# A two-block kernel: order of projections and indexer, place of the attention's halves, and the first tile's indexer queries

## Chip, cores and metric

The kernel runs as one program on one core of a Trainium2 chip. The metric is the device time of that core in microseconds (us), the median of three runs.

## What is computed

The reference is a chain of two transformer blocks on 512 tokens of width 1024, all in float32, with a final norm. The change lies in the attention of the first block and in what follows it up to the output projection:

```python
proj = rms_norm(h, norm1_g) @ w_in
q, k, v, qi, ki, wi, su, sv, ga, gb = split_columns(proj)
# dsa_attention, for each query:
rel = relu(einsum('bqhd,bsd->bqhs', qi, ki))       # the indexer: 8 heads of 64
score = einsum('bqh,bqhs->bqs', wi, rel)
score = where(causal, score, -inf)
_, sel = top_k(score, 128)                         # 128 = 512 // 4 keys for a query
logits = where(valid, q . k[sel] * 128 ** -0.5, -inf)
y_attn = softmax(logits) @ v[sel]
merged = sigmoid(ga) * (y_sgu @ w_branch_a) + sigmoid(gb) * (y_attn @ w_branch_b)
h = h + merged @ w_out
```

The queries of tokens 0 to 127 have at most 128 keys before them, so for them the selection takes every causal key. A mixture-of-experts layer, a second attention block (stick-breaking and linear attention) and a second mixture of experts follow; the change does not touch how they are computed.

## The kernel before

Four tiles of 128 tokens (t or i from 0 to 3) make up the 512 tokens. The program is a sequence of four stages: the first dense block (`dense1`), its experts, the second dense block, its experts and the final norm. A scheduler puts each engine's instructions in an order by their place in the program and by when it thinks they can run; each engine then works through its own list in order. Nothing jumps a queue on the chip.

In `dense1` each float32 product is made of three matmuls on high and low halves (`mm3`, lines 145 to 148): high by high, high by low, low by high. A projection takes 512 columns (or 256, or 328) of `w_in`: four chunks of 2 x 128 rows come by DMA from SP's queue into four raw buffers (`wr`), ACT rounds each to its high half (`wh`, L135), and VectorE, or GpSimd for the chunks listed in `POOLED`, subtracts to get the low half (`wl`, L138). TensorE then runs 4 tiles x 2 x 3 matmuls on each chunk, 96 for a projection, into four PSUM banks. What is done with the result is passed in as `evac`; for queries and keys it is the rope (L323 to L329, VectorE) and four transposes a tile (L504).

The order of these steps is written out by hand in `ORDER_A` (L32). q, k and V are projections of half the heads each (0 or 1). I0 and I1 are the indexer's projections: `ev_qi` (L445) rotates four heads' queries, transposes them and splits them into `qih` and `qil`; I1 also makes the keys `kih`, `kil` and the heads' weights `wi`. C1 to C3 are `choose(i)` (L467) for tile i: for each of 8 heads three score matmuls into one of three PSUM banks (`sp`), a Relu on ACT (L480), and an accumulation on VectorE (L477 for the first head, L481 for seven); then a causal mask on GpSimd (L483), 16 rounds on VectorE of maximum (L487) and replacement (L488), which take out 8 keys each, and a compare (L489) that writes the mask M[i]. There is no C0; M[0] is only causal. S0 and S1 are the gating unit's values, with statistics on VectorE (L568), H the attention heads, U and G further projections.

After the steps come the gating unit, branch a, the gate projection `sgb` and branch b. Branch b reads the attention's output as halves `yah`, `yal` in the pool `d1ya`: eight copies on ACT (L662) and eight subtractions on GpSimd (L663). Ahead of them in the program stands `later`, which loads vectors and calls `clear_rows` (L745): it fills a tile with zeros and copies it by two DMAs of GpSimd's queue over the two arrays `yd` in DRAM, which the experts later add to. That tile and a table of positions (`jp`) share a small temporary pool:

```python
with tc.tile_pool(name="gtmp", bufs=1, side="right", reuse_waits="tile") as tmp:
    front_consts(K, g, position_gap(K, tmp, pool_op), pool_op)
    clear_rows(K, tmp, pool_op)
```

The pool is placed at the right end of what is free. In a partition `jp` takes 512 bytes and the zeros 4096; a tile that is put where another one was waits for the readers of the old one.

Of the kernel before, what the change touches and what calls it, by code (L numbers as in the profile page):

```python
# [10 lines left out]
F32 = mybir.dt.float32  # L11
# [6 lines left out]
ALU = mybir.AluOpType  # L18
# [4 lines left out]
D = 1024  # L23
NT = T // 128
KD = D // 128
# [3 lines left out]
POOLED = (0, 1, 2) + tuple(range(16, 32))  # L29
LEFT1, LEFT2 = 3, 0  # L30
LAST1, LAST2 = 0, 3
ORDER_A = ("q0 I0 R I1 q1 C1 C2 V0 k0 C3 S0 S1 V1 H00 H01 H02 k1 H03 U0 H10 H11 H12 G0 H13 U1")  # L32
ORDER1 = ("turned",) * 2, ("logged",) * 2, ("logged",) * 2, ("ranked",) * 2
ORDER2 = ("last", "turned"), ("logged",) * 2, ("logged", "ranked"), ("ranked",) * 2
RING1, RING2 = 12, 15
# [4 lines left out]
def f32(ap):  # L40
    return ap.bitcast(F32)
# [10 lines left out]
def after(K, x, y):  # L52

    K.tc.add_manual_dep(x.ins, y.ins.name, mybir.DependencyInfo(mybir.DependencyClass.NoSync,
                                                                mybir.DependencyReason.DATA), reason="order")
# [12 lines left out]
def rsqrt(K, pool, a, n, name, keep=None):  # L68

    nc = K.nc  # L70

    def t_(role, dt=F32):
        return pool.tile([128, n], dt, name=f"{name}{role}", tag=f"rsq{n}{role}", bufs=2)

    sh = t_("s", I32)
    nc.vector.tensor_scalar(sh, a.bitcast(I32), 1, None, op0=ALU.logical_shift_right)
    yi = t_("i", I32)
    nc.vector.tensor_scalar(yi, sh, -1.0, float(0x5F3759DF), op0=ALU.mult, op1=ALU.add)
    y, c = yi.bitcast(F32), 1.0
    for i in range(3):  # L80

        t = t_(f"t{i}")
        if n == 1:
            nc.vector.tensor_scalar(t, y, y, a, op0=ALU.mult, op1=ALU.mult)
        else:
            nc.vector.tensor_mul(t, y, y)
            nc.vector.tensor_mul(t, t, a)
        y2 = keep if i == 2 and keep is not None else t_(f"y{i}")
        if i < 2:
            nc.vector.scalar_tensor_tensor(y2, t, 3.0 * c * c, y, op0=ALU.subtract, op1=ALU.mult)  # L90
            c = -2.0 * c ** 3
        else:
            nc.vector.tensor_scalar(t, t, -0.5 / c ** 3, 1.5 / c, op0=ALU.mult, op1=ALU.add)
            nc.vector.tensor_mul(y2, y, t)
        y = y2
    return y
# [12 lines left out]
class WStream:  # L109
# [18 lines left out]
    def split(self, raw, nk, n, into=None):  # L128
        nc, pool = self.K.nc, self.pool
        if into is None:  # L130
            wh = pool.tile([128, nk, n], F32R, name=f"wh{self.i}", tag="wh", bufs=self.nb)
            wl = pool.tile([128, nk, n], F32R, name=f"wl{self.i}", tag="wl", bufs=self.nb)
        else:
            wh, wl = into
        self.high = nc.scalar.activation(wh, raw, AF.Copy)  # L135
        pooled = self.i in self.pooled
        low = nc.gpsimd if pooled else nc.vector
        self.low = low.tensor_tensor(wl, raw, f32(wh), op=ALU.subtract)  # L138
        if pooled:
            self.pool_low = self.low  # L140
        self.i += 1
        return wh, wl


def mm3(nc, out, ah, al, bh, bl, first, last):
    nc.tensor.matmul(out, ah, bh, start=first, stop=False)  # L146
    nc.tensor.matmul(out, al, bh, start=False, stop=False)  # L147
    return nc.tensor.matmul(out, ah, bl, start=False, stop=last)  # L148
# [9 lines left out]
        return self.pool.tile(shape, dt, name=name, tag=self.tag, bufs=self.n)  # L158


def proj_tok(K, W, acc_pool, src, c0, n, xh, xl, evac):

    nc = K.nc
    accs = [acc_pool.tile([128, 512], F32, name=f"acc{t}", tag="acc", bufs=4) for t in range(NT)]
    for kc in range(4):
        raw = W.load(src, c0, n, 2 * kc, 2)
        wh, wl = W.split(raw, 2, n)
        for t in range(NT):
            for k in range(2):
                kk = kc * 2 + k  # L170
                mm3(nc, accs[t][:, :n], xh[:, kk, t * 128:(t + 1) * 128], xl[:, kk, t * 128:(t + 1) * 128],
                    wh[:, k, :], wl[:, k, :], kk == 0, kk == KD - 1)
            if kc == 3:
                evac(t, accs[t])

# [134 lines left out]
def rope(K, work, src, t, heads, half, name, out=None):  # L310

    nc = K.nc
    step = 64 // half
    cs = K.cos[:, t, ::step]
    sn = K.sin[:, t, ::step]
    ns = K.nsin[:, t, ::step]
    s4 = src.rearrange("p (h two d) -> p h two d", two=2, d=half)
    n = heads * 2 * half
    af = work.tile([128, 512], F32, name=name + "a", tag="rpa", bufs=2)[:, :n]
    bf = work.tile([128, 512], F32, name=name + "b", tag="rpb", bufs=2)[:, :n]  # L320
    a = af.rearrange("p (g d) -> p g d", d=half)
    b = bf.rearrange("p (h two d) -> p h two d", two=2, d=half)
    nc.vector.tensor_tensor(a, src.rearrange("p (g d) -> p g d", d=half),  # L323
                            cs[:, None, :].to_broadcast([128, heads * 2, half]), op=ALU.mult)
    nc.vector.tensor_tensor(b[:, :, 0, :], s4[:, :, 1, :], ns[:, None, :].to_broadcast([128, heads, half]), op=ALU.mult)
    nc.vector.tensor_tensor(b[:, :, 1, :], s4[:, :, 0, :], sn[:, None, :].to_broadcast([128, heads, half]), op=ALU.mult)
    if out is None:
        out = af
    nc.vector.tensor_tensor(out, af, bf, op=ALU.add)  # L329
    return out  # L330
# [38 lines left out]
def dense1(K, tc, A, later=None, router=None, dump=None):  # L369
    nc = tc.nc  # L370
    dump = dump or {}

    Q0, K0, V0, QI0, KI0, SU0, SV0, GA0, GB0 = 0, 1024, 2048, 3072, 3584, 3656, 4680, 5704, 6728
    w_in = A["w_in"][0]
    st = ExitStack()

    def P(name, stack=st, **kw):
        return stack.enter_context(tc.tile_pool(name=name, bufs=1, reuse_waits="tile", **kw))

    with st:  # L380
# [4 lines left out]
        W = WStream(K, wp)  # L385
# [6 lines left out]
        xh = xp.tile([128, KD, T], F32R, name="xh")  # L392
        xl = xp.tile([128, KD, T], F32R, name="xl")
        R = cst.tile([128, T], F32, name="n1R")
        with tc.tile_pool(name="d1x0", bufs=1, side="right", reuse_waits="tile") as x0:
# [19 lines left out]
            r = rsqrt(K, small, ss, NT, "n1r", cst.tile([128, NT], F32, name="n1rk"))  # L415
# [4 lines left out]
        accp = P("d1acc", space=PSUM)  # L420
# [5 lines left out]
        def block(name, dt=F32):  # L426
            return heap.tile([128, 4, 512], dt, name=name, tag="blk", bufs=HEAP)

        aw = ExitStack()
        work = P("d1k", aw)  # L430
# [5 lines left out]
        def split(hi, lo, x):  # L436
            nc.scalar.activation(hi, x, AF.Copy)
            nc.vector.tensor_sub(lo, x, f32(hi))


        qih, qil = block("qih", F32R), block("qil", F32R)
        kih, kil = (work.tile([128, T], F32R, name=n, tag=n, bufs=1) for n in ("kih", "kil"))
        wi = work.tile([128, NT, 8], F32, name="wi")

        def ev_qi(t, acc, g=0):  # L445
            qr = rope(K, work, acc[:, 0:256], t, 4, 32, f"rqi{g}{t}")
            ps = psq.tile([128, 4, 128], F32, name=f"qip{g}{t}")
            for j in range(2):
                nc.tensor.transpose(ps[:, j, :], qr[:, j * 128:(j + 1) * 128], K.ident)
            if g == 1:  # L450
                nc.vector.tensor_scalar(wi[:, t, :], acc[:, 320:328], r[:, t:t + 1], None, op0=ALU.mult)
                kr = work.tile([128, 128], F32, name=f"kir{t}", tag="kr", bufs=1)
                rope(K, work, acc[:, 256:320], t, 1, 32, f"rki{t}", kr[:, 0:64])
                nc.vector.tensor_copy(kr[:, 64:128], kr[:, 0:64])
                nc.tensor.transpose(ps[:, 2, :], kr, K.ident)
                split(kih[:, t * 128:(t + 1) * 128], kil[:, t * 128:(t + 1) * 128], ps[:, 2, :])
            s = (slice(None), slice(2 * g, 2 * g + 2), slice(t * 128, (t + 1) * 128))
            split(qih[s], qil[s], ps[:, 0:2, :])

        W.pooled = POOLED  # L460

        def index_projection(g):
            proj_tok(K, W, accp, w_in, QI0 + 256 * g, 328 if g else 256, xh, xl, lambda t, acc: ev_qi(t, acc, g))
            if g:
                after(K, nc.sync.dma_start(sgT_gain, A["sgu_norm_g"].rearrange("o (k p) -> p (o k)", p=128)), W.last)

# [145 lines left out]
        for i in range(1, NT):  # L612
            steps[f"C{i}"] = lambda i=i: choose(i)
        for name in ORDER_A.split():
            steps[name]()
        aw.close()
        with tc.tile_pool(name="d1y", bufs=1, reuse_waits="tile") as yp_:
# [10 lines left out]
            for gg in range(8):  # L628
                s_ = su[gg // 4][:, gg % 4, :]
                ps = psp.tile([128, 4, 128], F32, name=f"mx{gg}", tag="ps")  # L630
                for c in range(NT):
# [4 lines left out]
                                               op0=ALU.mult, op1=ALU.add)  # L636
# [56 lines left out]
        for t in range(NT):  # L693
            acc = accp.tile([128, 512], F32, name=f"acc{t}", tag="acc", bufs=4)
            s = slice(t * 128, (t + 1) * 128)
# [45 lines left out]
ROWS = 2 * T  # L741
# [2 lines left out]

def clear_rows(K, pool, behind):  # L745

    z = pool.tile([128, D], F32, name="zeros")
    after(K, K.nc.gpsimd.memset(z, 0.0), behind)
    for yd in K.yd:
        K.nc.gpsimd.dma_start(yd.rearrange("(a p) d -> p a d", p=128), z[:, None, :].to_broadcast([128, ROWS // 128, D]))  # L750


def moe_consts(K, pool):
# [1523 lines left out]
```

## Time and profile before

| what | value |
|---|---|
| median of the runs | 1777.3 us (1771.1 to 1876.48) |
| the profiled execution | 1777.42 us, its span 1775.7 us |
| TensorE matmuls (PE) | 1675.8 us busy, 94% |
| VectorE (DVE) | 813.6 us, 46% |
| ScalarE (ACT) | 522.5 us, 29% |
| GpSimd (POOL) | 293.2 us, 17% |
| DMA | 403.72 MB, mean 227 GB/s |
| mean granted TensorE clock | 0.983 |

Busy times are sums over the whole span, in which four stages with different limits follow each other. A matmul's time is that from its start to its modelled end; matmuls overlap, so the distance between the starts of neighbours is what one costs. An idle time in square brackets is the engine's wait before an instruction, and the arrow names what ended it.

### The profile page before, as it was taken

The numbers are of one execution on the slowest core, as the hardware profiler recorded it, in microseconds if no ns is written. First come the engines' busy times: TensorE is split into PE (matmuls) and PEld (weight loads), VectorE is DVE, ScalarE is ACT, GpSimd is POOL, SyncE is SP. The second block draws the span as 40 slices with busy tenths as digits, with TensorE's granted clock in tenths as the row PEclk, the third lists the DMA queues.
The fourth block names the chain that finished last, engine by engine and source line by source line (L and its number), as shares of the span: only waits on it lengthen the run. The fifth ranks groups of instructions, "written<-read, shape, count | busy, mean of one in ns | idle before, by whom it ended". The sixth has DMA issues, their size and how long they took to land. (4 is left out here: it accounts for less than half of the span.)

```text
span 1775.7 us, 22892 instructions
## 1 busy us (share of the span) xinstructions
PE 1675.8 (94%) x8958; PEld 1103.8 (62%) x8960; DVE 813.6 (46%) x1855; ACT 522.5 (29%) x898; POOL 293.2 (17%) x325
## 2 busy tenths in 40 slices
PE   6999999999999999999899999889999999999976
PEld 5977877788787844544387977688644353433423
DVE  4668846464345732322564278887611111211014
ACT  3333345663333311110245366634300000000002
POOL 1023301110221000000233357550000000000010
PEclk8989999999999999999999999999999999999998
DMA  4322221225722499999542220217499999999994
GB/s 128 105 60 83 84 83 48 60 84 146 284 83 79 185 420 403 420 419 418 220 129 63 81 72 2 72 37 292 189 420 419 420 419 419 419 419 420 418 418 155
DMA packets 112656, 403.72 MB, mean 227 GB/s; under 512 B 21950, under 2 KB 44478, under 8 KB 75936
## 3 DMA queue, kind: packets, MB, share of 16 engines
q1 hardware_dynamic: 102624, 376.63, 55.0%
q0 software_dynamic: 8880, 25.58, 3.8%
q8 instruction: 72, 1.18, 0.3%
q14 instruction: 40, 0.33, 0.1%
q10 hardware_dynamic: 1040, 0.00, 0.0%
HBM read 382.44 MB, written 27.26 MB: 231 GB/s over the span
## 5 line engine op out<-in xcount | busy, mean ns | idle before, releaser
L1465 PE MATMUL gg<-rg,xT 128*64 128x512 f32 x1536 | 374.3, 597 | 8.4 <-DMA rg<-in_w_expert_gate 4.5
L1465 PEld LDWEIGHTS gg<-rg,xT 128*64 128x64 f32 x1536 | 113.2, 136 | 211.5 <-issue 185.2
L1478 PE MATMUL py<-rg,aT 128*64 128x512 f32 x768 | 197.4, 605 | 20.5 <-DMA rg<-in_w_expert_down 20.5
L138 DVE TENSOR_TENSOR wl<-wr,wh 128x1024 fp32r<-128x1024 f32 (+2 forms) x97 | 121.8, 1258 | 161.8 <-ACT wh L135 160.8
L135 ACT ACTIVATE wh<-wr 128x1024 fp32r<-128x1024 f32 (+2 forms) x116 | 119.6, 1033 | 251.0 <-PE acc L148 119.2
L1478 PEld LDWEIGHTS py<-rg,aT 128*64 128x64 f32 x768 | 59.6, 139 | 138.8 <-issue 97.8
L1265 POOL DMA_INDIRECT yd<-ys,to x28 | 27.9, 997 | 655.6 <-DVE ys L1264 542.4
L1215 DVE SCALAR_TENSOR_TENSOR sg<-gg,gsl,sg 128x256 f32<-128x256 f32 (+1 forms) x32 | 19.7, 617 | 252.8 <-PE gg L1465 173.8
L146 PE MATMUL acc<-wh,xh 128*128 128x512 f32 (+2 forms) x320 | 123.8, 388 | 9.0 <-DVE xl L260 9.0
L148 PE MATMUL acc<-wl,xh 128*128 128x512 f32 (+2 forms) x320 | 123.4, 386 | 0.0
L147 PE MATMUL acc<-wh,xl 128*128 128x512 f32 (+2 forms) x320 | 123.3, 385 | 0.0
L1059 DVE TENSOR_TENSOR xT<-xp,gT 128x512 f32<-128x512 f32 x56 | 38.6, 690 | 152.6 <-PE xp L1056 151.5
L1226 ACT ACTIVATE aT<-ap 128x256 f32<-128x256 f32 (+1 forms) x32 | 15.7, 490 | 290.2 <-PE ap L1223 290.2
L1263 ACT ACTIVATE ys<-py,gsl 128x512 f32<-128x512 f32 x28 | 19.2, 687 | 258.3 <-PE py L1478 153.9
L1264 DVE TENSOR_SCALAR ys<-py,gsl 128x512 f32<-128x512 f32 x28 | 21.0, 751 | 135.0 <-PE py L1478 128.6
L146 PE MATMUL acc<-xh,wh 128*128 128x512 f32 x192 | 77.5, 404 | 0.0
L147 PE MATMUL acc<-xh,wl 128*128 128x512 f32 x192 | 76.7, 400 | 0.0
L148 PE MATMUL acc<-xl,wh 128*128 128x512 f32 x192 | 76.7, 399 | 0.0
L146 PEld LDWEIGHTS acc<-wh,xh 128*128 128x128 f32 x320 | 61.5, 192 | 21.1 <-DVE xl L260 9.2
L147 PEld LDWEIGHTS acc<-wh,xl 128*128 128x128 f32 x320 | 61.6, 193 | 12.0 <-issue 1.0
L148 PEld LDWEIGHTS acc<-wl,xh 128*128 128x128 f32 x320 | 61.5, 192 | 12.0 <-issue 0.5
L138 POOL TENSOR_TENSOR wl<-wr,wh 128x1024 fp32r<-128x1024 f32 x19 | 45.5, 2395 | 127.7 <-DVE wl L138 67.3
(790 smaller groups left out, 3552.8 us busy)
## 6 DMA issues: line engine op xcount, KB each, us to landing
rg<-in_w_expert_in SPq DMA_DIRECT2D x64, 1024.0 KB, 11.5
rg<-in_w_expert_gate SPq DMA_DIRECT2D x64, 1024.0 KB, 19.9
rg<-in_w_expert_up SPq DMA_DIRECT2D x64, 1024.0 KB, 20.3
rg<-in_w_expert_down SPq DMA_DIRECT2D x62, 1024.0 KB, 20.5
wr<-in_w_in SPq DMA_DIRECT2D x84, 512.0 KB, 3.6
rg<-in_w_expert_out SPq DMA_DIRECT2D x32, 1024.0 KB, 12.1
yd<-zeros POOLq DMA_DIRECT2D x2, 4096.0 KB, 21.4
yb<-yd POOLq DMA_DIRECT2D x16, 512.0 KB, 10.4
```

The source lines that it names most:

```text
L135: self.high = nc.scalar.activation(wh, raw, AF.Copy)
L138: self.low = low.tensor_tensor(wl, raw, f32(wh), op=ALU.subtract)
L146: nc.tensor.matmul(out, ah, bh, start=first, stop=False)
L147: nc.tensor.matmul(out, al, bh, start=False, stop=False)
L148: return nc.tensor.matmul(out, ah, bl, start=False, stop=last)
L1059: nc.vector.tensor_tensor(xT[:, k2 * 2:k2 * 2 + 2, :], ps, gT[:, kk:kk + 2, None].to_broadcast([128, 2, n]), op=ALU.mult)
L1215: K.gated = nc.vector.scalar_tensor_tensor(sg, ps_u, scale, sg, op0=ALU.mult, op1=ALU.mult)
L1263: nc.scalar.activation(y[:, 0:512], py[0], AF.Copy, scale=gate)
L1264: nc.vector.tensor_scalar(y[:, 512:D], py[1], gate, None, op0=ALU.mult)
L1265: nc.gpsimd.indirect_dma_start(yd, bass.IndirectOffsetOnAxis(ap=rows, axis=0), y, None, bounds_check=ROWS - 1, oob_is_err=False)
L1465: in_turn(nc.tensor.matmul(pss[i][64 * s:64 * s + 64, :], xT[kk // 4][:, kk % 4, c0 + 64 * s:c0 + 64 * s + 64], wt[2 * p + s, nm, kk // 4] ...
L1478: m = nc.tensor.matmul(py[q][64 * s:64 * s + 64, :], aT[:, f, 64 * s:64 * s + 64], wt[2 * p + s, second, f // 2][:, f % 2, q * 512:(q + 1) ...
```

## The change

The order of steps in `ORDER_A` is another: V0 stands ahead of C1, and k0 and S0 ahead of C2 and C3. The order of the projections among each other is as it was, and so are the chunks that GpSimd splits. `proj_tok` takes a range of columns for the first tile: I0 leaves it out, and I1 computes only the 64 columns of the indexer's key for it; `ev_qi` leaves out the rope, transposes and splits of its queries and its weights. `clear_rows` fills a tile of half the width, 2048 bytes a partition, and writes the same zeros from it in rows of half the length, with eight neighbouring rows of `yd` from one partition.

```diff
--- before.py
+++ after.py
@@ -29,7 +29,7 @@
 POOLED = (0, 1, 2) + tuple(range(16, 32))
 LEFT1, LEFT2 = 3, 0
 LAST1, LAST2 = 0, 3
-ORDER_A = ("q0 I0 R I1 q1 C1 C2 V0 k0 C3 S0 S1 V1 H00 H01 H02 k1 H03 U0 H10 H11 H12 G0 H13 U1")
+ORDER_A = ("q0 I0 R I1 q1 V0 C1 k0 S0 C2 C3 S1 V1 H00 H01 H02 k1 H03 U0 H10 H11 H12 G0 H13 U1")
 ORDER1 = ("turned",) * 2, ("logged",) * 2, ("logged",) * 2, ("ranked",) * 2
 ORDER2 = ("last", "turned"), ("logged",) * 2, ("logged", "ranked"), ("ranked",) * 2
 RING1, RING2 = 12, 15
@@ -158,7 +158,7 @@
         return self.pool.tile(shape, dt, name=name, tag=self.tag, bufs=self.n)
 
 
-def proj_tok(K, W, acc_pool, src, c0, n, xh, xl, evac):
+def proj_tok(K, W, acc_pool, src, c0, n, xh, xl, evac, cols=None):
 
     nc = K.nc
     accs = [acc_pool.tile([128, 512], F32, name=f"acc{t}", tag="acc", bufs=4) for t in range(NT)]
@@ -166,10 +166,13 @@
         raw = W.load(src, c0, n, 2 * kc, 2)
         wh, wl = W.split(raw, 2, n)
         for t in range(NT):
+            lo, hi = cols if cols and t == 0 else (0, n)
             for k in range(2):
                 kk = kc * 2 + k
-                mm3(nc, accs[t][:, :n], xh[:, kk, t * 128:(t + 1) * 128], xl[:, kk, t * 128:(t + 1) * 128],
-                    wh[:, k, :], wl[:, k, :], kk == 0, kk == KD - 1)
+                if lo == hi:
+                    break
+                mm3(nc, accs[t][:, lo:hi], xh[:, kk, t * 128:(t + 1) * 128], xl[:, kk, t * 128:(t + 1) * 128],
+                    wh[:, k, lo:hi], wl[:, k, lo:hi], kk == 0, kk == KD - 1)
             if kc == 3:
                 evac(t, accs[t])
 
@@ -443,24 +446,31 @@
         wi = work.tile([128, NT, 8], F32, name="wi")
 
         def ev_qi(t, acc, g=0):
-            qr = rope(K, work, acc[:, 0:256], t, 4, 32, f"rqi{g}{t}")
+
+            if t == g == 0:
+                return
             ps = psq.tile([128, 4, 128], F32, name=f"qip{g}{t}")
-            for j in range(2):
-                nc.tensor.transpose(ps[:, j, :], qr[:, j * 128:(j + 1) * 128], K.ident)
+            if t:
+                qr = rope(K, work, acc[:, 0:256], t, 4, 32, f"rqi{g}{t}")
+                for j in range(2):
+                    nc.tensor.transpose(ps[:, j, :], qr[:, j * 128:(j + 1) * 128], K.ident)
+            if g == 1 and t:
+                nc.vector.tensor_scalar(wi[:, t, :], acc[:, 320:328], r[:, t:t + 1], None, op0=ALU.mult)
             if g == 1:
-                nc.vector.tensor_scalar(wi[:, t, :], acc[:, 320:328], r[:, t:t + 1], None, op0=ALU.mult)
                 kr = work.tile([128, 128], F32, name=f"kir{t}", tag="kr", bufs=1)
                 rope(K, work, acc[:, 256:320], t, 1, 32, f"rki{t}", kr[:, 0:64])
                 nc.vector.tensor_copy(kr[:, 64:128], kr[:, 0:64])
                 nc.tensor.transpose(ps[:, 2, :], kr, K.ident)
                 split(kih[:, t * 128:(t + 1) * 128], kil[:, t * 128:(t + 1) * 128], ps[:, 2, :])
-            s = (slice(None), slice(2 * g, 2 * g + 2), slice(t * 128, (t + 1) * 128))
-            split(qih[s], qil[s], ps[:, 0:2, :])
+            if t:
+                s = (slice(None), slice(2 * g, 2 * g + 2), slice(t * 128, (t + 1) * 128))
+                split(qih[s], qil[s], ps[:, 0:2, :])
 
         W.pooled = POOLED
 
         def index_projection(g):
-            proj_tok(K, W, accp, w_in, QI0 + 256 * g, 328 if g else 256, xh, xl, lambda t, acc: ev_qi(t, acc, g))
+            proj_tok(K, W, accp, w_in, QI0 + 256 * g, 328 if g else 256, xh, xl, lambda t, acc: ev_qi(t, acc, g),
+                     cols=(256, 320) if g else (0, 0))
             if g:
                 after(K, nc.sync.dma_start(sgT_gain, A["sgu_norm_g"].rearrange("o (k p) -> p (o k)", p=128)), W.last)
 
@@ -744,10 +754,12 @@
 
 def clear_rows(K, pool, behind):
 
-    z = pool.tile([128, D], F32, name="zeros")
+    w = D // 2
+    z = pool.tile([128, w], F32, name="zeros")
     after(K, K.nc.gpsimd.memset(z, 0.0), behind)
     for yd in K.yd:
-        K.nc.gpsimd.dma_start(yd.rearrange("(a p) d -> p a d", p=128), z[:, None, :].to_broadcast([128, ROWS // 128, D]))
+        K.nc.gpsimd.dma_start(yd.rearrange("(p a) d -> p (a d)", p=128).rearrange("p (a d) -> p a d", d=w),
+                              z[:, None, :].to_broadcast([128, 2 * ROWS // 128, w]))
 
 
 def moe_consts(K, pool):
```

## Rows read from the trace of the kernel before

**Rows 1.** Page, part 2: busy tenths of the 40 slices of the span.

```profile
PE   6999999999999999999899999889999999999976
...
DMA  4322221225722499999542220217499999999994
```

**Rows 2.** Chain that ended last: start us, us, what.

```profile
1705.35 23.23 DMA rg<-in_w_expert_down
```

**Rows 3.** Timeline of PE, end of I0: start us, us, engine line op out<-in xcount.

```profile
52.87 0.29 PE L146 MATMUL acc<-wh,xh 128*128 128x256 f32 x1
...
53.23 0.28 PE L146 MATMUL acc<-wh,xh 128*128 128x256 f32 x1
```

**Rows 4.** Timeline of PE at 389 us, matmuls of 128 columns.

```profile
388.86 2.84 PE L632 MATMUL mx<-sgc,hres 128*128 128x128 f32 x24
```

**Rows 5.** Timeline of PE from q1's end to V0's steady part.

```profile
99.42 0.40 PE L146 MATMUL acc<-wh,xh 128*128 128x512 f32 x1
...
123.54 0.39 PE L146 MATMUL acc<-wh,xh 128*128 128x512 f32 x1
...
124.24 0.39 PE L146 MATMUL acc<-wh,xh 128*128 128x512 f32 x1
```

**Rows 6.** Groups of PE between 99.42 and 123.54, by shape: busy us, mean ns, idle before.

```profile
L148 PE MATMUL acc<-wl,xh 128*128 128x512 f32 x9 | 5.1, 564 | 0.0
...
L148 PE MATMUL sp<-kil,qih 64*128 64x384 f32 x8 | 3.5, 518 | 0.0
...
L148 PE MATMUL sp<-kil,qih 64*128 64x256 f32 x8 | 2.6, 339 | 0.0
...
L504 PE MATMUL qp<-ident,rq12a 128*128 128x128 f32 x4 | 0.6, 280 | 1.1 <-DVE rq12a L329 1.1
```

**Rows 7.** Windows: PE, PEld, DVE, ACT, POOL busy (x), PEclk, DMA share, GB/s.

```profile
105.00:110.00 5.00, 4.55 (x15) 3.03 (x16) 3.32 (x8) 0.98 (x2) 0.00 (x0) 0.62 0.38 110
110.00:115.00 5.00, 5.00 (x20) 3.67 (x19) 1.95 (x4) 1.92 (x5) 0.00 (x0) 0.50 0.00 0
```

**Rows 8.** Timeline of DVE in the rope of q1.

```profile
98.82 0.68 DVE L329 TENSOR_TENSOR rq10a<-rq10a,rq10b 128x512 f32<-128x512 f32 x1
...
103.22 2.08 DVE L329 TENSOR_TENSOR rq12a<-rq12a,rq12b 128x512 f32<-128x512 f32 x1
```

**Rows 9.** Timeline of POOL at the same time.

```profile
102.38 2.36 POOL L138 TENSOR_TENSOR wl<-wr,wh 128x1024 fp32r<-128x1024 f32 x1 [3.55 <-ACT wh L135]
```

**Rows 10.** Groups of PE between 164.71 and 172, k0's end.

```profile
L504 PE MATMUL kp<-ident,rk02a 128*128 128x128 f32 x4 | 0.6, 280 | 1.7 <-DVE rk02a L329 1.7
```

**Rows 11.** Timeline of DVE in the rounds of C3.

```profile
177.97 0.69 DVE L487 MAX8 m<-sc 128x8 f32<-128x512 f32 x1 [0.40 <-POOL sc L483]
...
196.07 0.68 DVE L568 BATCH_NORM_STATS2 svs<-hres 128x6 f32<-128x512 f32 x1
196.67 0.68 DVE L487 MAX8 m<-sc 128x8 f32<-128x512 f32 x1
...
204.10 0.92 DVE L489 TENSOR_SCALAR M<-sc 128x512 f32<-128x512 f32 x1
```

**Rows 12.** Timeline of PE at the start of branch b.

```profile
479.49 0.40 PE L148 MATMUL acc<-xl,wh 128*128 128x512 f32 x1
482.12 0.50 PE L146 MATMUL acc<-yah,wh 128*128 128x512 f32 x1 [2.24 <-ACT yah L662]
...
488.73 0.39 PE L146 MATMUL acc<-yah,wh 128*128 128x512 f32 x1
```

**Rows 13.** Timeline of ACT at the same time.

```profile
481.45 4.26 ACT L662 ACTIVATE yah<-ya 128x512 fp32r<-128x512 f32 x8
```

**Rows 14.** Timeline of POOL from 430 to 496 us.

```profile
458.91 1.86 POOL L750 DMA_DIRECT2D yd<-zeros  x2 [0.30 <-POOL zeros L748]
...
487.40 5.08 POOL L663 TENSOR_TENSOR yal<-ya,yah 128x512 fp32r<-128x512 f32 x4 [0.20 <-DMA yd<-zeros]
```

**Rows 15.** DMA issues from 457 to 490 us: KB each, median us to landing.

```profile
wr<-in_w_in SPq DMA_DIRECT2D x3, 512.0 KB, 8.8
```

## The prediction

> **What bounds the kernel.** I read the slices of the page first. TensorE is nine tenths busy or more in nearly all slices up to the 27th (about 45 us each) but for a dip around the 23rd, the DMA engines are full in slices 15 to 19 and from slice 30 on [rows 1]: dense block, expert block, dense block, expert block, each bound by one thing. The chain of waits ends in the last expert block, where one weight load follows another, 23.23 us for a down block at 1705.35 [rows 2]. A load there begins when the work before it has freed its place, so the two dense blocks set when the loads start: what TensorE saves in the first dense block comes off the end one for one, as long as nothing later has slack. Everything below is therefore priced on TensorE between 40 and 490 us. There the windows and the timelines show two holes, at 99 to 124 us and at 479 to 489 us; all else is matmuls back to back.
>
> All sums go against the profiled execution, 1777.42 us (span 1775.7 and 1.7 around it), which lies 0.1 above the median of the runs.
>
> **1. No indexer queries for tokens 0 to 127.** In I0 this removes 4 chunks x 2 rows x 3 = 24 matmuls of 256 columns. Two such lines three starts apart, 52.87 and 53.23 [rows 3], give 0.12 each: 2.9 us. In I1 24 matmuls shrink from 328 columns (estimate 0.12 x 328/256 = 0.154) to 64. No row has 64 columns with 128 rows in front. The nearest is 24 matmuls of 128 columns in 2.84 us [rows 4], less a tail of about 0.2: 0.11 each. I take 0.11: 24 x 0.044 = 1.0. Bounds: no cheaper than 0.12 (0.7), or a quarter of 0.12 (2.9). Four transposes at 0.11 go too: 0.4. Sum 4.3 (3.9 to 6.2). The rope, the splits on ACT and VectorE and the one multiply that go with them run beside matmuls: nothing. The loads and weight splits of both projections stay, so nothing is late next but the same matmuls of the other three tiles.
>
> **2. The order.** Before, C1 and C2 stand between q1 and V0. From the first transpose's neighbour at 99.42 to the steady matmuls at 123.54 pass 24.12 us [rows 5]. In it lie 24 wide matmuls, 24 score matmuls of 384 columns and 24 of 256 (8 of each line; the ninth wide one of its row began earlier) and four transposes of each of four tiles [rows 6]. At the spacing of the wide matmuls after it, 0.70 for three (123.54 to 124.24), and for 384 columns three quarters of that, this is 24 x 0.233 + 24 x 0.175 + 24 x 0.12 + 16 x 0.11 = 14.4 us. Lost: 9.7, of which 1.1 is a wait for the rotated queries [rows 6]; the rest is the clock, granted at 0.62 and then 0.50 [rows 7], the lower level, entered after that wait among short matmuls.
>
> After the change V0's wide matmuls follow q1, C1's scores come between V0 and k0, and C2's and C3's between S0 and S1, where no rope and no transposes stand. Not all of the 9.7 comes back. The wait of 1.1 is the rope's last addition taking 2.08 instead of 0.68 us [rows 8]: it lasts to 105.30, just past a GpSimd weight split that ran from 102.38 to 104.74 [rows 9]. V0's splits remain on GpSimd next to q1's rope, so I leave that 1.1 in, and likewise the 1.7 of k0's rope [rows 10], which costs nothing new. The same clash is new for the 21 score accumulations, each with two operands in SBUF as that addition has: before, C1's and C2's fell between GpSimd's splits. One split (2.4) may hold each of the three C's. Three PSUM banks hold scores ahead, some 3 x 3 x 0.175 = 1.6 us of TensorE's work, so about 0.8 shows: 2.4 for three. Net 9.7 - 1.1 - 2.4 = 6.2. Bounds: 11.4 if also both rope waits (1.1 is in the 9.7, so plus 1.7) go; below, rival A.
>
> Steps moved: 72 score matmuls, 21 Relu, 24 accumulations, 3 masks on GpSimd, 48 rounds of maximum and replacement, 3 final compares; no DMA. They pass V0, k0 and S0, not a queue of SP. On VectorE the rounds of C3 took from 177.97 to 205.02 [rows 11], 27 us; C2's, scaled by 384/512, take 20. Where they fall after the change: q1's wide matmuls end 4 us earlier than 99.4, and V0, k0 and S0 (96 matmuls each, 22.4 us), the transposes (3.5), C1's scores (2.9) and the waits (3.6) bring TensorE to about 172, and C2's and C3's scores to about 180. S1 ends near 206 and V1 near 228. The rounds of C2 and C3 then last from 180 to 227, and some ten later with other work between them. Who waits for M3: the last tile of the first head, some ten us behind V1's end. The cover is nearly used up there, but not short: 0. Who is queued behind the rounds: V1's first low halves at about 206, which stay on VectorE. Between two rounds other work gets in: the statistics at 196.07 ran between a replacement and the maximum at 196.67 [rows 11]. So 0.
>
> **3. The halves of the attention's output and the zeros.** TensorE issues its last gate matmul at 479.49 and is steady again at 488.73 [rows 12]: 9.24 us for 16 steps worth 16 x 0.233 = 3.7. Lost: 5.5, which begins with a wait of 2.24 on the high halves. These are eight copies on ACT from 481.45 [rows 13], though the last head, which writes their source, lies a whole branch earlier. On GpSimd the clearing of yd was issued at 458.91, and the last four subtractions wait for it until 487.40 [rows 14]: the old zeros tile of 4 KB a partition lies in part where the fourth half goes. With 2 KB the two don't overlap, by my layout of the tiles, and the zeros themselves no longer wait for branch a's halves. Then the copies (4.26 us of ACT, between its weight splits) and the subtractions (10.2 of an empty GpSimd) run under the gate projection: gain 5.5, bounds 0 (rival B) and 5.5.
>
> The write of zeros moves to about 380 to 400 us, when the last head's tiles are free. It is the same 8.39 MB from half the source, in pieces half as long, and took 28 us (458.91 to 487.40). It now meets the reload of x and the first loads of branch a. While it ran before, the weight loads landed in 8.8 us [rows 15] and TensorE did not wait, since four raw buffers of 24 x 0.233 = 5.6 us each lie ahead. So 0. Without that cover: rival D. Nothing reads yd before the first expert block. The memset is half as long, and the iota before it earlier: 0.
>
> **Sum** 4.3 + 6.2 + 5.5 = 16.0: 1777.4 - 16.0 = 1761.4. I say 1761.
>
> **Rivals.**
> A. The loss moves along with the C's. For it: C2 and C3 still stand together, 48 short matmuls with waits of VectorE among them, and light work with a wait is what came before the drop in [rows 7]. Against: C3 alone, with a wait of 1.7, kept its pace. Then part 2 is 9.7 - 9.7 - 2.4 = -2.4, and the time 1770.
> B. The copies of part 3 stay late, because what held them is not the zeros. For: ACT's copies wait on no space that the zeros touch, only their order does. 1761.4 + 5.5 = 1767.
> C. GpSimd's splits hold each C in full: 3 x 2.4 shows, nothing is covered by the banks. Part 2 is 9.7 - 1.1 - 7.2 = 1.4: 1766. The Trainium skill, "SBUF — State Buffer", section "SBUF: two separate sides", says that VectorE's and GpSimd's common port pair is locked for a whole instruction and the other fully blocks; the addition of 2.08 us agrees.
> D. The zeros choke the loads. The row order changes: a partition now writes eight rows in a run, with a distance of 32 KB between partitions instead of 4. If loads land one in 8.8 us for longer than 4 / (1/5.6 - 1/8.8) = 62 us, TensorE waits; at 84 us (three times 28) it is 15 - 4 - 9.5 = 1.5 loads short, 13 us: 1774. For: that write order is in no row. Against: 28 us would have to double. The Trainium skill, "DMA: Bandwidth & Descriptors", section "Latency and other measured facts", has copies at 207 GB/s for a pitch of 512 KiB and 103 for 4 MiB; by the latter the write would take 81 us, but 32 KiB isn't in its list.
> E. Slower: the rounds of C2 and C3 leave no gap. They end at about 227; V1 needs its first low halves at about 206 and waits 21 us, with some 2 for a clock that falls in the wait: 1761.4 + 23 = 1784. It decides as soon as the low halves lie behind the last round in VectorE's order. [Rows 11] speak against it.
> F. The gain is given back: the first expert block's loads are bound by DMA and could start no earlier. Against: they start when places come free. 1777.
>
> **Chances.** Forecast 0.52, A 0.20, B 0.07, C 0.07, D 0.04, E 0.05, F 0.05. The forecast's own range is 1754 (6.2 + 11.4 + 5.5 = 23.1 off) to 1766. The range 1753 to 1775 takes in A to C and part of D, and leaves out E, F. A 2% difference, about what runs of this kernel can tell from none, is 35.5: faster than 1741.8 needs more than all bounds together, 0.03; slower than 1812.8 needs more than E, 0.02; within, 0.95.
>
> **What would show it.** Part 1: 24 matmuls fewer in I0, and q1's begin 4 us earlier. Part 2: full clock from V0 to S1 and no piece like 99 to 124; rounds of C2 and C3 on VectorE up to about 235 with V1's splits between them. If the clock falls near S0 or S1, it is A; an accumulation of 2 us beside a split is C. Part 3: copies to the halves before 475 and no wait at the first matmul of branch b; the zeros near 390 us. Wrong would be a wait of V1, of the first head's last tile, or of branch a's first weights.

## The result, and the profile after

The changed kernel takes 1785.35 us in the median (1785.04 to 1788.29, four runs) where the kernel before takes 1775.03 beside it: ratio 1.0064, 95% interval 1.0045 to 1.0084, some 11 us slower. One of the four runs of the kernel before took 1876.48 us, in a slower state that a run falls into now and then, and the ratio goes by the others. Forecast was 1761, with a range of 1753 to 1775. The profiled execution took 1785.42 us, its span 1783.7.

Where the 8.0 us between the spans come from is read from five places of TensorE's timeline: the first matmuls of q1, V1, k1, branch a and the output projection. First the kernel before (start us, us, instruction):

```profile
77.31 0.39 PE L146 MATMUL acc<-wh,xh 128*128 128x512 f32 x1
...
217.97 0.40 PE L146 MATMUL acc<-wh,xh 128*128 128x512 f32 x1
...
240.51 0.48 PE L146 MATMUL acc<-wh,xh 128*128 128x512 f32 x1
...
412.43 0.40 PE L146 MATMUL acc<-ysh,wh 128*128 128x512 f32 x1
...
552.51 0.39 PE L146 MATMUL acc<-wh,mh 128*128 128x512 f32 x1
```

The same five in the changed kernel:

```profile
71.99 0.39 PE L146 MATMUL acc<-wh,xh 128*128 128x512 f32 x1
...
215.46 0.39 PE L146 MATMUL acc<-wh,xh 128*128 128x512 f32 x1
...
254.14 0.48 PE L146 MATMUL acc<-wh,xh 128*128 128x512 f32 x1
...
426.19 0.40 PE L146 MATMUL acc<-ysh,wh 128*128 128x512 f32 x1
...
561.54 0.39 PE L146 MATMUL acc<-wh,mh 128*128 128x512 f32 x1
```

Up to q1 the change gains 5.3. From q1 to V1 it loses 2.8 (143.5 against 140.7), in V1, which here means from V1's first matmul to k1's, 16.1 (38.7 against 22.5), from k1 to branch a 0.1, and from there to the output projection it gains 4.7. Sum: 9.0 later, and nearly all of it is there at the end. So parts 1 and 3 did about what was forecast, and part 2, the order, cost 18.9 instead of gaining 6.2.

The loss in V1 is one wait. TensorE issues the first head's first scores at 228.53 and then nothing until a low half comes:

```profile
228.53 0.38 PE L543 MATMUL lg<-kT,qT 128*128 128x128 f32 x2
242.44 0.80 PE L148 MATMUL acc<-wl,xh 128*128 128x512 f32 x1 [13.53 <-DVE wl L138]
```

VectorE's timeline shows the four low halves of V1 (`wl`, L138) and where they stand among the rounds (`MAX8` of 384 columns is C2, of 512 C3):

```profile
205.37 1.23 DVE L138 TENSOR_TENSOR wl<-wr,wh 128x1024 fp32r<-128x1024 f32 x1 [2.34 <-ACT wh L135]
...
211.40 1.21 DVE L138 TENSOR_TENSOR wl<-wr,wh 128x1024 fp32r<-128x1024 f32 x1
...
217.94 0.69 DVE L497 MAX8 m<-sc 128x8 f32<-128x512 f32 x1
...
241.17 1.22 DVE L138 TENSOR_TENSOR wl<-wr,wh 128x1024 fp32r<-128x1024 f32 x1
...
243.81 1.22 DVE L138 TENSOR_TENSOR wl<-wr,wh 128x1024 fp32r<-128x1024 f32 x1
...
246.65 0.42 DVE L499 TENSOR_SCALAR M<-sc 128x512 f32<-128x512 f32 x1
```

Two came in good time. The third stands behind 14 of C3's 16 rounds, and VectorE gets to it at 241.17, though ACT had its high half done by 217:

```profile
215.48 1.06 ACT L135 ACTIVATE wh<-wr 128x1024 fp32r<-128x1024 f32 x1 [0.53 <-PE acc L147]
```

M3 is written at 246.65, where the forecast had the rounds end at about 235. The windows (busy us of PE, PEld, DVE, ACT, POOL, then the granted clock) tell the rest:

```profile
176.00:182.00 6.00, 4.93 (x27) 3.40 (x26) 4.84 (x7) 3.59 (x7) 2.37 (x1) 1.00 0.36 109
182.00:196.00 14.00, 14.00 (x39) 9.52 (x38) 12.29 (x24) 6.48 (x12) 2.91 (x4) 0.52 0.07 26
196.00:228.00 32.00, 32.00 (x138) 25.73 (x137) 29.04 (x84) 9.30 (x11) 3.28 (x4) 1.00 0.17 50
228.00:242.00 14.00, 0.91 (x5) 0.59 (x4) 14.00 (x46) 0.99 (x1) 0.00 (x0) 0.70 0.00 0
242.00:250.00 8.00, 7.56 (x23) 6.00 (x24) 7.82 (x22) 1.55 (x3) 0.00 (x0) 0.67 0.51 141
```

From 228 to 242 VectorE works without a gap while TensorE stands. The clock is at its lower level in two stretches: from 182 to 196, among the scores of C2 and C3, behind a wait of 0.89, and from inside the long wait until about 5 us after it. Here is the wait in front of the first:

```profile
180.89 0.44 PE L146 MATMUL sp<-kih,qih 64*128 64x384 f32 x1 [0.89 <-ACT rl L490]
```

Where C1 and C2 had stood the clock is now up, but the drop of [rows 7] has a successor. The rope's last addition still takes 2.29 us beside a split (0.68 and 2.08 in [rows 8]), and k0's 2.34.

Part 3 went as forecast. The zeros go out at 403.93, the halves are made from 471.14, and branch b begins at 494.27 with no wait, 0.24 behind the last gate matmul; in [rows 12] it waited 2.24. The write took longer to land (24.5 us against 21.4), and the first loads of branch a 16.3; TensorE did not wait for them.

```profile
403.93 2.33 POOL L761 DMA_DIRECT2D yd<-zeros  x2 [0.30 <-POOL zeros L759]
```

```profile
471.14 4.28 ACT L672 ACTIVATE yah<-ya 128x512 fp32r<-128x512 f32 x8 [4.31 <-PE acc L147]
```

```profile
494.03 0.40 PE L148 MATMUL acc<-xl,wh 128*128 128x512 f32 x1
494.27 0.39 PE L146 MATMUL acc<-yah,wh 128*128 128x512 f32 x1
```

### The profile page after: what moved, and what is told of

The parts are those of the page before. It is cut to its first block, busy times and chain, and to the rows that moved or that the text cites. A ratio compares the mean times of both kernels' runs of the same rounds, so it can differ in the third digit from the quotient of the medians.

```text
span 1783.7 us, 22830 instructions
## 1 busy us (share of the span) xinstructions
PE 1671.4 (94%) x8932; PEld 1102.5 (62%) x8932; DVE 811.9 (46%) x1844; ACT 522.0 (29%) x896; POOL 294.1 (16%) x325
## 5 line engine op out<-in xcount | busy, mean ns | idle before, releaser
L138 DVE TENSOR_TENSOR wl<-wr,wh 128x1024 fp32r<-128x1024 f32 (+2 forms) x97 | 127.1, 1314 | 141.9 <-ACT wh L135 141.4
L148 PE MATMUL acc<-wl,xh 128*128 128x512 f32 (+3 forms) x312 | 120.9, 390 | 13.5 <-DVE wl L138 13.5
L146 PE MATMUL acc<-wh,xh 128*128 128x512 f32 (+3 forms) x312 | 121.1, 389 | 8.4 <-DVE xl L263 8.4
L147 PE MATMUL acc<-wh,xl 128*128 128x512 f32 (+3 forms) x312 | 121.1, 388 | 0.0
L1071 DVE TENSOR_TENSOR xT<-xp,gT 128x512 f32<-128x512 f32 x56 | 38.7, 690 | 152.5 <-PE xp L1068 151.4
L138 POOL TENSOR_TENSOR wl<-wr,wh 128x1024 fp32r<-128x1024 f32 x19 | 45.4, 2391 | 133.6 <-ACT wh L135 124.5
## 6 DMA issues: line engine op xcount, KB each, us to landing
yd<-zeros POOLq DMA_DIRECT2D x2, 4096.0 KB, 24.5
```

The costliest lines, as they stand in the source:

```text
L1071: nc.vector.tensor_tensor(xT[:, k2 * 2:k2 * 2 + 2, :], ps, gT[:, kk:kk + 2, None].to_broadcast([128, 2, n]), op=ALU.mult)
```

## Experiments

Ratios are to the kernel before, with 95% intervals; the changed kernel's is 1.0064.

**The order taken back.** Changed kernel, with

```diff
-ORDER_A = ("q0 I0 R I1 q1 V0 C1 k0 S0 C2 C3 S1 V1 H00 ...
+ORDER_A = ("q0 I0 R I1 q1 C1 C2 V0 k0 C3 S0 S1 V1 H00 ...
```

> The changed kernel with the old order of steps: parts 1 and 3 alone. Theory: in the changed kernel's trace the skipped queries bring q1's first matmul forward from 77.31 to 71.99 us (5.3), and branch b's start loses 4.7 us less; nothing else is in this kernel. So 1775.0 - 10.0 = 1765, 3 us either way, ratio 0.994. Rival (parts 1 and 3 do not reach the end, or the zeros' new place hurts): 1775, ratio 1.00.

Measured 1769.03 us, 0.9961 (0.9944 to 0.9977): 7 us faster than before. Parts 1 and 3 reach the end, with some 3 less than the traces show; the interval reaches to 10.

**The order alone**, the same edit the other way round on the kernel before.

> The kernel before with the new order of steps alone: part 2. Theory: between q1's and V1's first matmul 2.8 us more, and V1 16.1 us longer because its low halves stand in VectorE's order behind the rounds of C2 and C3: 1775.0 + 18.9 = 1794, 4 us either way, ratio 1.011, and a wait of TensorE of some 13 us in V1 that a low half ends. Rival (the loss needs the skipped queries or the zeros' new place): below 1785.

Measured 1795.69 us, 1.0117 (1.0081 to 1.0152), and V1's wait is 13.52 us, ended by a low half. The loss is the order's, and needs nothing else of the change.

```profile
247.05 0.80 PE L148 MATMUL acc<-wl,xh 128*128 128x512 f32 x1 [13.52 <-DVE wl L138]
```

**V1's low halves on GpSimd.**

```diff
-POOLED = (0, 1, 2) + tuple(range(16, 32))
+POOLED = (0, 1, 2) + tuple(range(16, 36))
```

> The changed kernel with the low halves of V1's four chunks on GpSimd instead of VectorE, so that nothing of V1 waits in VectorE's order; the rounds stay where they are. Theory (V1's low halves queue behind the rounds): the wait of 13.5 us and the clock's fall after it go, V1 lasts 22.5 us as before instead of 38.7: 1785.4 - 16 = 1769, 4 us either way, ratio to before 0.997. Rival (the masks of C2 and C3 themselves are what is late): the wait only moves to the first head's transposes, and the time stays within 4 us of 1785.

Measured 1778.64 us, 1.0021 (1.0006 to 1.0036). That is 7 to 8 us of the 16, between theory and rival. V1 itself lasts 22.5 us, as the theory had it, but k1's first low half stands in the same queue and TensorE waits there; from k1 to branch a it takes 179.9 us instead of the changed kernel's 172.1. First TensorE, then VectorE:

```profile
246.79 0.79 PE L148 MATMUL acc<-wl,xh 128*128 128x512 f32 x1 [3.89 <-DVE wl L138]
```

```profile
245.06 0.42 DVE L499 TENSOR_SCALAR M<-sc 128x512 f32<-128x512 f32 x1
...
245.52 1.21 DVE L138 TENSOR_TENSOR wl<-wr,wh 128x1024 fp32r<-128x1024 f32 x1
```

Not V1's low halves are late, but all that VectorE has to do behind the rounds. The next run tests that.

**Half of the rounds.**

```diff
-            for q in range(16):
+            for q in range(16 if i < 2 else 8):
```

> The changed kernel with 8 instead of 16 rounds of maximum and replacement in C2 and C3; it leaves out half of the selection of tiles 2 and 3. VectorE's list is 8 x 1.25 + 8 x 1.52 = 22 us shorter, the scores on TensorE are as they were. Theory (VectorE's whole queue is late, not V1's low halves alone): V1 lasts 22.5 us and k1 and the heads after it wait for nothing: 1785.4 - 16 = 1769, 4 us either way, about 9 below the run with V1's low halves on GpSimd. Rival (the time between V1 and branch a is set by something else than VectorE): 1778, as with the low halves on GpSimd.

Measured 1770.61 us, 0.9977 (0.9961 to 0.9992): 0.9% or 15 us below the changed kernel, as the theory says, and 8 below the run with the low halves moved. V1 lasts 22.5 us and k1 waits for no low half. The first matmuls of V1 and k1:

```profile
213.13 0.40 PE L146 MATMUL acc<-wh,xh 128*128 128x512 f32 x1
...
235.67 0.48 PE L146 MATMUL acc<-wh,xh 128*128 128x512 f32 x1
```

The rounds of C2 and C3, begun one projection before they were wanted, are the cause.

**The C's apart.** Changed kernel, order V0 C1 k0 C2 S0 C3 S1 V1.

> The changed kernel with C2 moved from behind S0 to behind k0 and C3 left alone behind S0 (order V0 C1 k0 C2 S0 C3 S1 V1), so that the rounds of C2 fall in the 17 us in which VectorE was idle during S0. Theory: VectorE is done with the rounds before V1's third low half is wanted, V1 lasts 22.5 us, and the 48 short score matmuls no longer stand together, so the clock stays up: 1785.4 - 16 - 6 = 1763, 5 us either way, ratio 0.993. Rival (the scores beside GpSimd's splits and k0's rope cost as much wherever they stand): V1's 16 come back and nothing else, 1769; and if the clock falls at each C, 1775 or more.

Measured 1771.63 us, 0.997 (0.9949 to 0.9992). V1's 16 are back (it lasts 22.7), but the clock was granted at 0.91 between 125 and 185 us and at 0.83 up to 205: the rival.

**C2 behind V0.** Changed kernel, order C1 V0 C2 k0 C3 S0 S1 V1.

> The changed kernel with the order C1 V0 C2 k0 C3 S0 S1 V1: C1 and C3 where they were before the change, C2 moved from beside C1 to behind V0, so no two C's stand together and VectorE is done with all rounds before S1 ends. Theory (two C's side by side, with TensorE waiting among short matmuls, bring the clock down): full clock between q1 and S1, and as good as the old order or up to 4 us better: 1765 to 1769. Rival (each group of score matmuls brings it down wherever it stands): 1772 or more.

Measured 1772.28 us, 0.9987 (0.9970 to 1.0004), the clock 0.94 between 125 and 185, where it fell behind waits of 1.32 and 0.72. Missed: keeping the C's apart does not hold the clock up.

**Part 1 alone and part 3 alone**, on the kernel before.

> The kernel before with the skipped queries alone: part 1. Theory: 5.3 us, as q1's first matmul in the changed kernel: 1775.5 - 5.3 = 1770, 3 us either way. Rival (the work left out was cover for something, or the clock gives it back): 1774 or more.

> The kernel before with the new clearing of rows alone: part 3. Theory: the copies to the halves run under the gate projection and branch b starts 4.7 us sooner: 1775.5 - 4.7 = 1771, 3 us either way; with the skipped queries alone it adds up to the run of both. Rival (the wait was not on the way to the end): 1775.

Measured 1772.80 us, 0.9993 (0.9977 to 1.0008), and 1772.55 us, 0.9989 (0.9975 to 1.0003). The traces show both gains: 4.7 us up to q1 in the first, 4.9 from branch a to the output projection in the second. The medians show only 1.3 and 2.0, each by itself not told from nothing. That raised the question what else differs between executions.

**Two splits off GpSimd.** The old order with parts 1 and 3, with and without

```diff
-POOLED = (0, 1, 2) + tuple(range(16, 32))
+POOLED = (0, 1, 2) + tuple(i for i in range(16, 32) if i not in (18, 26))
```

> The changed kernel with the old order of steps (parts 1 and 3 alone), and the third weight split of V0 and of S0 on VectorE instead of GpSimd: the two that run beside the rope of q1 and k0. Theory (GpSimd's subtraction holds VectorE's addition of two operands in SBUF): that addition takes 0.68 us for rq12 and rk02 instead of 2.1, the waits of 1.1 and 1.7 before the transposes go, and against the old order with parts 1 and 3 the time falls by 1 to 2.8, to about 0.995 of before. Rival (the addition waits for something else, a semaphore say): it stays at 2 us, and the time is the same or 1 to 2 us longer for the two splits on VectorE.

> The changed kernel with the old order of steps once more, in more rounds and beside the run with two splits moved: is it faster than the kernel before by the 5.3 + 4.7 us that the traces show, or by the 3.3 that the runs of the two parts alone add up to? Theory (each part saves what its trace shows; what the runs show less is where the clock happened to fall): between the two, ratio 0.994 to 0.997. Rival (the parts gain nothing together): 0.999 or more.

Measured 1761.47 us, 0.9918 (0.9903 to 0.9934), against 1769.62 us, 0.9966 (0.9950 to 0.9982), for the same kernel without it. This is the fastest version, 14 us below the kernel before, and two subtractions are worth 8. VectorE's timeline of the faster one: the addition is back at 0.68, and the split follows it.

```profile
98.08 0.68 DVE L332 TENSOR_TENSOR rq12a<-rq12a,rq12b 128x512 f32<-128x512 f32 x1
...
100.73 1.22 DVE L138 TENSOR_TENSOR wl<-wr,wh 128x1024 fp32r<-128x1024 f32 x1
```

Its windows, with the granted clock third from the right:

```profile
95.00:125.00 30.00, 29.64 (x143) 21.76 (x142) 26.40 (x72) 12.22 (x22) 5.71 (x4) 1.00 0.22 70
125.00:185.00 60.00, 59.47 (x261) 45.51 (x260) 54.24 (x117) 23.58 (x32) 22.73 (x12) 1.00 0.26 79
```

and those without the edit:

```profile
95.00:125.00 30.00, 28.89 (x114) 21.07 (x113) 22.89 (x57) 10.10 (x20) 5.37 (x4) 0.72 0.13 38
125.00:185.00 60.00, 58.14 (x248) 44.13 (x247) 50.11 (x111) 19.48 (x26) 23.71 (x12) 0.94 0.25 78
```

The waits without the edit, in front of the transposes of q1 and of k0:

```profile
100.33 0.75 PE L514 MATMUL qp<-ident,rq12a 128*128 128x128 f32 x4 [1.11 <-DVE rq12a L332]
...
163.69 0.63 PE L514 MATMUL kp<-ident,rk02a 128*128 128x128 f32 x4 [1.68 <-DVE rk02a L332]
```

With the edit the first is gone and the second is down to 0.36, and the clock does not fall. That the clock is the larger part is seen in the profile of the very same kernel in the first experiment, the order taken back. It has both waits, 1.09 and 1.69, but there the clock did not fall:

```profile
95.00:125.00 30.00, 28.85 (x142) 21.19 (x141) 26.98 (x69) 11.27 (x21) 8.32 (x6) 1.00 0.17 53
125.00:185.00 60.00, 58.14 (x260) 44.87 (x259) 54.68 (x117) 22.47 (x30) 24.50 (x12) 1.00 0.26 80
```

From q1 to V1 that profile takes 134.3 us, against 143.5 with the waits and the fallen clock and 133.4 with neither: here the waits by themselves cost 1 us and the clock 9. So a wait does not bring the clock down each time.

**The same two splits in the kernel before and in the changed one.**

> The kernel before with the third weight split of V0 and of S0 on VectorE instead of GpSimd, and nothing else. Theory (the wait of 1.1 and 1.7 of the transposes behind the held addition is what lets the clock fall near C1, C2 and C3, in some executions more than in others): both waits go, the clock stays at the upper level from 95 to 205 us, and the time falls by the same 8 that it fell by with parts 1 and 3 in: 1775.1 - 8 = 1767, 3 us either way, ratio 0.9955, with a narrow spread. Rival (the short score matmuls themselves bring the clock down, the waits only add 2.8): 1772.

> The changed kernel, with its order, and the same two splits on VectorE. Theory (the new order has a loss of its own, VectorE's queue of two groups of rounds in front of V1's low halves, which the two splits don't touch): the wait of 13 us in V1 stays, of the other waits only the rope's go: 1785.4 - 4 = 1781, 4 us either way, ratio 1.004. Rival (the new order suffers only from the held additions and would win without them): below 1768.

Measured 1769.35 us, 0.9971 (0.9955 to 0.9987): 5 us with an interval of 2 to 8, between theory and rival. In the profile the first wait is gone, the second 0.36, and the clock is 1.00 from 72 to 260 us. And 1780.93 us, 1.0031 (1.0016 to 1.0045): 6 below the changed kernel, with V1's wait at 14.43 and the clock at 0.90 between 125 and 185, where waits of 0.79 and 0.90 for a Relu stand among the scores of C1 and C2. The order loses without the rope's waits too.

The two kernels with the old order and the splits moved differ by parts 1 and 3 alone: 1761.47 against 1769.35, 7.9 us, or 9.4 by the two ratios. Where these waits are out, the medians show about what the traces show.

One number shows the lot for the two orders: the time from q1's to V1's first matmul in each profile.

| order | from q1 to V1, us |
|---|---|
| old, splits on GpSimd, five profiles | 134.3, 137.1, 140.7, 143.5, 143.6 |
| old, two splits moved, two profiles | 133.4, 133.5 |
| new, splits on GpSimd, four profiles | 140.4, 143.2, 143.5, 144.4 |
| new, two splits moved | 138.2 |

## Why the prediction was wrong

- **"Who is queued behind the rounds: V1's first low halves at about 206, which stay on VectorE. ... So 0."** This step failed, and with it the sign. From the statistics that ran between two rounds in [rows 11] I took that other work gets in between. It does where VectorE's list has it there, and the list is fixed before the kernel runs: two low halves stood early, the third behind 14 of C3's rounds. I had asked whether VectorE would take another instruction, not whether it would be in time; busy from 206 to 250 us without room, it was 13.5 late. Rival E named the mechanism, its place and nearly its price (21 and 2; measured 16.1), at a chance of 0.05. It decides a little sooner than I wrote: not all low halves have to stand behind the last round.
- **"The cover is nearly used up there, but not short: 0."** M3 came at 246.65, some 10 us later than the 235 to 237 I put it at. I started C2's rounds at 180; they began at 186.7, since TensorE came to C2's scores at 176.4 and not at 172, and the last of them ran at the lower clock. VectorE's other work between the rounds took some 13 us where I allowed ten. With 20 + 27 us of rounds ahead of two projections of 22.4 there was no slack to be late with.
- **Part 2's 9.7 lost.** The sum of 14.4 at full clock was too short. The 24 wide matmuls and what lies among them, 24.12 us in [rows 5], take 17.9 at full clock with the wait of 1.09 (the order taken back, the lines below) and 17.2 without it (the two profiles with the splits moved). So the clock took 6.2 there, not 8.6. And I took one profile's drop for a fixed cost of where C1 and C2 stand. In the old order the clock costs between nothing and some 9 from q1 to V1, by execution; that C3 kept its pace, which I held against rival A, was luck of that profile, for in three of the other four with the waits in the clock falls at C3. What has to go is the wait that I left in at 1.1: with the two splits moved no profile of the old order shows a drop. So the order took away nothing lasting, and gave the clock another place to fall: rival A, at 0.20, which came along with E. I had treated the rivals as if one excluded the other.

```profile
95.83 0.40 PE L146 MATMUL acc<-wh,xh 128*128 128x512 f32 x1
...
113.74 0.39 PE L146 MATMUL acc<-wh,xh 128*128 128x512 f32 x1
```

- **Held accumulations, 2.4.** Waits of 0.23, 0.78 and 0.89 us at scores, for the score multiply once and the Relu twice: 1.9, the right size. Rival C is out. The rule of the locked port pair in the Trainium skill, "SBUF — State Buffer", section "SBUF: two separate sides", agrees with the two moved splits (2.08 to 0.68 us), and what hung on it was not rival C but the clock.
- **Part 1, 4.3.** Measured 5.3 between the two traces. One pair is not sharp: q1 begins between 71.99 and 73.84 us in the ten profiles without the queries and between 76.77 and 77.82 in the four with them, 4.4 apart in the mean, which is the forecast. The median of part 1 alone shows less (1.3, with an interval of 4.1 faster to 1.4 slower).
- **Part 3, 5.5.** Measured 4.7 and 4.9 in the traces. The halves wait for nothing of the zeros any more, so rival B is out, and the zeros' write, though 24.5 instead of 21.4 us to land, stopped nobody: rival D is out. By the same numbers no slow-pitch effect of the size in the Trainium skill, "DMA: Bandwidth & Descriptors", section "Latency and other measured facts", shows here.
- **One for one to the end** held: 9.0 us at the output projection, 8.0 in the span, and in all 14 profiles 1222 to 1226 us pass from there to the end. Rival F is out.
- **The slices.** The dip that I read around TensorE's 23rd slice stands at the 20th and at the 26th and 27th [rows 1]. Nothing hung on it.

Open: why the clock falls behind some of these waits and not behind others; why the two splits gave 8 us in one kernel and 5 in the kernel before (with an interval of 2 to 8); and why parts 1 and 3 each alone show less in the medians than in the traces. That the clock falls by chance at the remaining waits fits the last two, but no run shows it by itself.

## What to carry to other kernels

Before moving a long chain on a helper engine past work that bounds the kernel, add up all that this engine has to do until each of its consumers needs something, and compare it with the bound engine's time up to there; a row in which something got in between says only where the list had it. Read a clock drop in a profile by what came before it, and look for the short wait that it begins with: here moving two subtractions of 2.4 us gained 8 us in one kernel and 5 in another, about as much as the two parts of the change that worked (6 to 7 together). A loss seen in one profile is a fixed cost only when a second profile has it too.

## What the runs showed of the hardware

A subtraction on GpSimd holds an addition on VectorE that has both operands in SBUF until it is done (2.08 us instead of 0.68). The compare that writes M[1] took 1.88 us beside such a subtraction in the changed kernel and 0.28 without one in the kernel before, though no run moved that split. A round's maximum beside one keeps its 0.43 us (256 columns). First GpSimd, then VectorE:

```profile
132.90 2.40 POOL L138 TENSOR_TENSOR wl<-wr,wh 128x1024 fp32r<-128x1024 f32 x1 [3.93 <-ACT wh L135]
...
144.09 2.40 POOL L138 TENSOR_TENSOR wl<-wr,wh 128x1024 fp32r<-128x1024 f32 x1 [3.19 <-ACT wh L135]
```

```profile
133.93 0.43 DVE L497 MAX8 m<-sc 128x8 f32<-128x256 f32 x1
...
144.76 1.88 DVE L499 TENSOR_SCALAR M<-sc 128x256 f32<-128x256 f32 x1
```

In the 14 profiles the granted clock goes from 1.0 to 0.5, the level of 1.2 GHz, 24 times between 60 and 270 us, for 4 to 18 us. Each time it began during a wait of TensorE (the shortest 0.72 us) or within 2.5 us after one; 16 other waits of 0.78 to 1.71 us passed without a fall. Where V0's wide matmuls follow q1, the wait of 1.4 to 1.5 us in q1's rope brought it down in none of five profiles; in the old order, where the scores of C1 and C2 follow q1, the wait of 1.1 did in three of five.

Beside the run with the two splits moved, the 15 runs of the kernel before go from 1771.6 us at a mean granted clock of 0.987 to 1780.2 at 0.979; its own six runs lie between 1761.3 and 1763.1, at 0.985 to 0.989.
